# Feed-forward output of an encoder layer: sixteen of 22 row tiles by seven quadrant products per pair, partial sums kept in DRAM

## Chip, cores and metric

The kernel runs on one core of a Trainium2 chip. The core has TensorE (PE; PEld is its weight load), VectorE (DVE), ScalarE (ACT), GpSimd (POOL) and SyncE (SP), whose queue issues all the DMA transfers named here. The metric is device microseconds of one execution; each version is run several times, and the median is given.

## The reference, cut to what matters

One encoder layer is computed for two sequences of 512 tokens with a model width of 1024: a state-space branch, a differential-attention branch and a cross-attention branch, merged with gates, and a feed-forward part. All is in float32. The change touches only the last product:

```python
x = x + merged @ p['w_out'][l]
xn2 = _rmsnorm(x, p['norm_ffn'][l])
gate, up = jnp.split(xn2 @ p['w_ffn_in'][l], 2, axis=-1)
return x + (jax.nn.silu(gate) * up) @ p['w_ffn_out'][l]      # D_FF = 2816
```

After it `_rmsnorm(x, norm_final)` gives the output.

## The kernel before, in words

Features lie on the 128 partitions, the 1024 tokens of both sequences (NT) on the columns, 512 (L) per sequence. The feed-forward width of 2816 is KFF = 22 tiles of 128 rows; the output has KD = 8 tiles of rows, m = 0 to 7.

Float32 products are made from halves: `split` (L106) writes a rounded high half with ACT (L109, or L112 with a scale) and the rest, the low half, with DVE (L110 or L113). Each product of a 128x128 weight with 512 columns is then three matmuls: high by high, high by low, low by high (`mm3`, L124, and `product`, L732).

**First product (gate and up), L768 to L805.** It uses a seven-product scheme for 2x2 quadrants. One quadrant index is the sequence (columns 0:512 or 512:1024), the other on the input side is the upper or lower half of the eight input tiles (tiles i and i + 4), and on the output side the gate or the up tile. `operands` (L656) builds for each of four input pairs seven operands (four quadrants taken as they are or differenced with DVE and POOL, L663 to L666) and their high and low halves, in the buffers th0, tl0, th1, tl1 (two each, so four pairs fill them all). `weights4` (L677) loads the two weight tiles and forms four sums with POOL (L695 to L698) and splits all. One iteration has seven products (`SEVEN`, L741) of four k with three matmuls: 84 matmuls. `products` (L743) gives each a PSUM bank, in the middle iterations one product after the other; in the first and the last iteration k is the outer loop, with seven banks open. Sums of the products (`summed`, L776) are made by DVE from PSUM. Then the gate: DVE L800, L803, L804, ACT L801, POOL L802, and the tile of 128 x 1024 goes to DRAM (`aD`, L805).

**Second product, L825 to L867.** It is plain. The 22 row tiles are read back from `aD` in blocks of FBLK = 3, 5, 7 and 7 (L830) and split (L832) into "aa" or "ab" buffers. For each block and each m the weight columns are loaded and split (`weight`, L115), and `mm3` multiplies them with both sequences. The first block copies PSUM to `y` with ACT (L860), later ones add with DVE (L862); in the second block POOL adds the residual x1, which had been put into DRAM (L846, L847). The last block is done in three parts of columns (512, 256, 256) with its weights kept, so that the final norm of a part (`final`, L815, with sums of squares from L146) runs beside the next part.

**What sets the order.** The kernel is written with a tile framework: it takes the program's instructions with their dependencies and schedules them per engine at build time. At run time each engine's queue, SP's too, is in order, and an instruction that waits holds up all behind it. Buffers are pooled by tag: "ld" has four of 128 x 1024, "wf" two, the weight halves two each, "mm" six PSUM banks and "tr" two. A buffer is given out again when all its readers are done.

Of the kernel before, what the change touches and what calls it, by code (L numbers as in the profile page):

```python
# [10 lines left out]
F32 = mybir.dt.float32  # L11
# [18 lines left out]
T = 8  # L30
NC = L // T
G = 32
FBLK = (3, 5, 7, 7)


NG = (7, 5, 7)
# [12 lines left out]
def encoder(ctx: ExitStack, tc: tile.TileContext, a, out):  # L49
# [37 lines left out]
    def aux():  # L87
        return bank("tr")
# [556 lines left out]
    def out_tile(m, s, w):  # L645
# [7 lines left out]
        nc.sync.dma_start(x1D[m, :, cs], x1[m][:, cs])  # L653
        sum_sq(accs[s], x1[m][:, cs], m == 0)

    def operands(i):  # L656

        xa_, xb_ = x1[i], x1[i + 4]
        S.activation(out=xa_, in_=xa_, func=AF.Copy, scale=vcol("norm_ffn", i))
        V.tensor_scalar_mul(xb_, xb_, vcol("norm_ffn", i + 4))  # L660
        b11, b12, b21, b22 = xa_[:, 0:L], xa_[:, L:NT], xb_[:, 0:L], xb_[:, L:NT]
# [4 lines left out]
        V.tensor_tensor(out=t_[:, 3], in0=b21, in1=t_[:, 1], op=ALU.subtract)  # L666
        j = i // 2
        th, tl = slot(f"th{j}", [P, 7, L], F32R, "th"), slot(f"tl{j}", [P, 7, L], F32R, "tl")
        split(th[:, 0], tl[:, 0], b11)
        split(th[:, 1:3].rearrange("p a n -> p (a n)"), tl[:, 1:3].rearrange("p a n -> p (a n)"), xb_)  # L670
        split(th[:, 3:5], tl[:, 3:5], t_[:, 0:2])
        split(th[:, 5:7], tl[:, 5:7], t_[:, 2:4])
        return th, tl

    H = 4 * P

    def weights4(i):  # L677

        a1, a2 = (wp.tile([P, DM], F32, tag="wf", name="wf") for _ in range(2))
        nc.sync.dma_start(a1, a["w_fg"][i])  # L680
        nc.sync.dma_start(a2, a["w_fu"][i])
# [12 lines left out]
        s12, s34 = (slot("ws", name="ws") for _ in range(2))  # L694
        PO.tensor_tensor(out=s12[:, :H], in0=a2[:, :H], in1=a2[:, H:], op=ALU.add)  # L695
        PO.tensor_tensor(out=s12[:, H:], in0=s12[:, :H], in1=a1[:, :H], op=ALU.subtract)
        PO.tensor_tensor(out=s34[:, H:], in0=a1[:, H:], in1=s12[:, H:], op=ALU.subtract)
        PO.tensor_tensor(out=s34[:, :H], in0=a1[:, :H], in1=a2[:, :H], op=ALU.subtract)  # L698
        yield
        sp(ap2, s12, "s", "S1", "S2")  # L700
        sp(ap2, s34, "s", "S3", "S4")
        yield
# [14 lines left out]
            out_tile(m, s, w)  # L717
    phase.close()
    open_tags(phase, th1=2, tl1=2, ws=2)
    w0 = weights4(0)  # L720
    res0 = next(w0)
    next(w0)
    ops.append(operands(2))
    ops.append(operands(3))
    ses.close()
    ap2 = phase.enter_context(tc.tile_pool(name="ffn", bufs=1, reuse_waits="tile"))
    next(w0)

# [11 lines left out]

    SEVEN = (("A11", 0), ("S2", 4), ("A12", 1), ("S3", 5), ("S1", 3), ("A22", 6), ("S4", 2))  # L741

    def products(i, w):  # L743


        if i == 0:
            ps = [bank() for _ in range(6)]
            for j, k in ((0, 0), (0, 1), (1, 0), (1, 1), (0, 2), (1, 2), (0, 3), (1, 3)):
                for p_, (nm, o) in zip(ps, SEVEN):
                    if nm[0] == "AS"[j]:  # L750
                        product(p_, w[nm], o, (k,))
            yield from ps
            last = bank()
            product(last, w["S4"], 2)
            yield last
        elif i == KFF - 1:
            ps = [bank() for _ in range(6)] + [aux()]
            for k in range(4):
                for p_, (nm, o) in zip(ps, SEVEN):
                    product(p_, w[nm], o, (k,))  # L760
            yield from ps
        else:
            for nm, o in SEVEN:
                p_ = bank()
                product(p_, w[nm], o)
                yield p_

    for i in range(KFF):  # L768
        w = res0
        if i > 0:  # L770
            wg = weights4(i)
            w = next(wg)
            next(wg)
            next(wg)

        def summed(tag, p_, other, bufs=1):  # L776
            t_ = ap2.tile([P, L], F32, tag=tag, name=tag, bufs=bufs)
            V.tensor_tensor(out=t_, in0=p_, in1=other, op=ALU.add)  # L778
            return t_

        ps = products(i, w)
# [5 lines left out]
        p1 = ap2.tile([P, L], F32, tag="p1", name="p1")  # L787
        S.copy(p1, p0)
        u2 = summed("u2", next(ps), p1)
        gf0 = summed("gf", next(ps), p1, 2)  # L790
        u3 = summed("u3", next(ps), u2)
        p5 = next(ps)
        u4 = summed("p1", p5, u2)
        up1 = summed("up", p5, u3, 2)
        up0 = summed("up", next(ps), u3, 2)
        gf1 = summed("gf", next(ps), u4, 2)
        ac = ap2.tile([P, NT], F32, tag="ac", name="ac")
        for s, gf, up in ((0, gf0, up0), (1, gf1, up1)):
            cs = slice(s * L, (s + 1) * L)
            V.tensor_tensor(out=gf, in0=gf, in1=accs[s], op=ALU.mult)  # L800
            S.activation(out=ac[:, cs], in_=gf, func=AF.Tanh, scale=0.5)  # L801
            PO.tensor_tensor(out=up, in0=up, in1=accs[s], op=ALU.mult)  # L802
            V.scalar_tensor_tensor(out=ac[:, cs], in0=ac[:, cs], scalar=1.0, in1=gf, op0=ALU.add, op1=ALU.mult)  # L803
            V.tensor_tensor(out=ac[:, cs], in0=ac[:, cs], in1=up, op=ALU.mult)  # L804
        nc.sync.dma_start(aD[i], ac)  # L805
    phase.close()
    tes.close()


    open_tags(phase, yo=4)  # L810
    aes = ExitStack()
    open_tags(aes, side="right", aa=14, ab=14)
    y, y2 = [], []

    def final(acc, c0, n):  # L815
# [9 lines left out]
    f0 = 0  # L825
    for bi, nb in enumerate(FBLK):
        ah, al = [], []
        for i in range(f0, f0 + nb):
            ac = slot("ld", name="fl")
            nc.sync.dma_start(ac, aD[i])  # L830
            th, tl = (slot(("aa", "ab")[i // 7 % 2], [P, NT], F32R, n_) for n_ in ("ah", "al"))
            split(th, tl, ac, scale=0.5)  # L832
            ah.append(th)
            al.append(tl)
        last, kept = bi == len(FBLK) - 1, {}

        for parts in (((0, L),), ((L, L // 2),), ((L + L // 2, L // 2),)) if last else (((0, L), (L, L)),):
            acc = new_acc() if last else None
            for m in range(KD):
                if bi == 0:  # L840
                    if m % 2 == 0:
                        y2.append(slot("yo", [P, 2, NT], name=f"y{m}"))
                    y.append(y2[-1][:, m % 2])
                elif bi == 1:
                    xr = slot("ld", name="xr1")
                    nc.sync.dma_start(xr, x1D[m])  # L846
                    PO.tensor_tensor(out=y[m], in0=y[m], in1=xr, op=ALU.add)  # L847
                wsrc = a["w_fo"][m, :, f0 * P : (f0 + nb) * P]
                if not last:
                    wh, wl = weight(wsrc, nb * P)  # L850
                elif m in kept:
                    wh, wl = kept[m]
                else:
                    kept[m] = wh, wl = weight(wsrc, nb * P, "ab" if m < 6 else None)
                o = [bank()[:, :n] for _, n in parts]
                for k in range(nb):
                    mm3(o, wh, wl, [(ah[k][:, c : c + n], al[k][:, c : c + n]) for c, n in parts], k, nb)
                for o_, (c, n) in zip(o, parts):
                    if bi == 0:
                        S.copy(y[m][:, c : c + n], o_)  # L860
                    else:
                        V.tensor_tensor(out=y[m][:, c : c + n], in0=y[m][:, c : c + n], in1=o_, op=ALU.add)  # L862
                    if last:
                        sum_sq(acc, y[m][:, c : c + n], m == 0, n, V if m == KD - 1 else PO)
            if last:
                final(acc, *parts[0])
        f0 += nb  # L867

    phase.close()
    aes.close()  # L870
# [398 lines left out]
```

## Time and profile before

| | |
|---|---|
| runs of the kernel before | 1673.69 us median of 3 (1670.11 to 1674.54) |
| profiled execution: its time, its span | 1674.95 us, 1673.2 us |
| mean granted TensorE clock | 0.989 |
| first product: writes of its 22 tiles | issued from 1028.3 to 1433.7 us |
| second product and final norm | about 1418 us to the end |

The profile shows one execution. The page gives each engine's busy time and, at its part 4, the chain of work that ended last. Windows give busy time and counts by engine and stretch; the timeline lists instructions with start, duration, line, and output and input tiles; "x4" after a row means that many merged. A group's row gives its total us, the mean ns of one, and the idle time ahead of it with what ended it. Matmuls overlap, so a matmul's own duration is a latency; the distance from one to the next is what counts.

### The profile page before, as it was taken

How to read it: one execution, taken by the hardware profiler on the slowest of the kernel's cores; microseconds unless marked ns; L12 is line 12 of the kernel's file. 1: busy time of each engine (PE TensorE's matmuls, PEld its weight loads, DVE VectorE, ACT ScalarE, POOL GpSimd, SP SyncE). 2: the span in 40 equal slices, each digit the busy share in tenths (PEclk: the TensorE clock that was granted, in tenths of full speed). 3: DMA queues.
4: the chain of work that ended last, by engine and by line, in shares of the span. 5: the costliest groups of instructions: out<-in, count | busy, mean ns of one | idle time of the engine just before them, and what ended most of it. 6: DMA issues, size and time to landing. Idle time of an engine off the chain costs nothing.

```text
span 1673.2 us, 21052 instructions
## 1 busy us (share of the span) xinstructions
PE 1625.6 (97%) x7916; PEld 1357.8 (81%) x7916; DVE 1076.2 (64%) x1788; ACT 622.1 (37%) x1092; POOL 391.7 (23%) x253
## 2 busy tenths in 40 slices
PE   5999999999999999999999999999999999999997
PEld 4788887888897788878888878888888888888887
DVE  7946898154554776777655668777777777743324
ACT  6534412245343456554323443223323223421121
POOL 0001000000001121120243346555554552500021
PEclk9999999999999999999999999999999999999999
DMA  9343252747111221333554432322222223741302
GB/s 367 114 154 127 96 170 89 222 174 241 46 57 64 88 57 40 112 107 120 182 187 127 140 101 79 125 87 82 83 86 79 88 79 115 252 133 52 84 17 101
DMA packets 79269, 197.69 MB, mean 118 GB/s; under 512 B 11072, under 2 KB 26688, under 8 KB 79168
## 3 DMA queue, kind: packets, MB, share of 16 engines
q1 hardware_dynamic: 79168, 196.35, 35.4%
q8 instruction: 62, 1.02, 0.3%
q14 instruction: 39, 0.32, 0.1%
HBM read 141.82 MB, written 50.30 MB: 115 GB/s over the span
## 4 chain that ended last, share of the span: by engine, by line
PE 79%; DVE 11%; DMA 3%; issue 2%; ACT 2%; POOL 1%; SPq 1%; DVEq 0%; POOLq 0%; ACTq 0%
PE bkmm L129 15%; PE bkmm L132 15%; PE bkmm L130 15%; PE bkmm L738 8%; PE bkmm L737 8%; PE bkmm L739 8%; DVE st L1140 1%; DVE wl L110 1%; PE bktr L1122 1%; POOL mg L587 1%; PE bksc L533 1%; DMA c_n<-cD 1%; PE bksc L534 1%; PE bkmm L438 1%; PE bkmm L439 1%
## 5 line engine op out<-in xcount | busy, mean ns | idle before, releaser
L109 ACT CAST wh<-wf 128x1024 fp32r<-128x1024 f32 (+4 forms) x164 | 142.3, 868 | 385.4 <-PE bkmm L130 225.9
L132 PE MATMUL bkmm<-xh,wl 128*128 128x512 f32 x640 | 252.1, 394 | 3.0 <-DVE wl L110 3.0
L129 PE MATMUL bkmm<-xh,wh 128*128 128x512 f32 x640 | 251.8, 393 | 2.3 <-DVE t L505 1.2
L130 PE MATMUL bkmm<-xl,wh 128*128 128x512 f32 x640 | 251.7, 393 | 0.0
L738 PE MATMUL bkmm<-tl,wh 128*128 128x512 f32 x612 | 240.1, 392 | 2.5 <-DVE tl L110 2.5
L737 PE MATMUL bkmm<-th,wh 128*128 128x512 f32 x612 | 239.9, 392 | 0.0
L739 PE MATMUL bkmm<-th,wl 128*128 128x512 f32 x612 | 238.5, 391 | 0.0
L110 DVE TENSOR_TENSOR wl<-wf,wh 128x1024 fp32r<-128x1024 f32 (+4 forms) x164 | 175.7, 1072 | 94.5 <-ACT wh L109 93.9
L129 PE MATMUL bkmm<-ah,wh 128*128 128x512 f32 (+1 forms) x408 | 147.1, 361 | 0.2 <-ACT wh L109 0.2
L130 PE MATMUL bkmm<-al,wh 128*128 128x512 f32 (+1 forms) x408 | 147.0, 360 | 0.0
L132 PEld LDWEIGHTS bkmm<-xh,wl 128*128 128x128 f32 x640 | 120.7, 189 | 29.1 <-DVE wl L110 3.8
L129 PEld LDWEIGHTS bkmm<-xh,wh 128*128 128x128 f32 x640 | 120.7, 189 | 28.7 <-DVE t L505 2.6
L130 PEld LDWEIGHTS bkmm<-xl,wh 128*128 128x128 f32 x640 | 120.5, 188 | 24.7 <-issue 0.4
L506 POOL TENSOR_TENSOR t<-t,rs 128x512 f32<-128x512 f32 x16 | 24.6, 1537 | 494.5 <-DVE t L505 494.5
L738 PEld LDWEIGHTS bkmm<-tl,wh 128*128 128x128 f32 x612 | 115.8, 189 | 28.1 <-DVE tl L110 4.2
L737 PEld LDWEIGHTS bkmm<-th,wh 128*128 128x128 f32 x612 | 115.8, 189 | 24.4 <-ACT th L109 0.3
L739 PEld LDWEIGHTS bkmm<-th,wl 128*128 128x128 f32 x612 | 115.5, 189 | 24.0
L132 PE MATMUL bkmm<-ah,wl 128*128 128x512 f32 (+1 forms) x408 | 127.4, 360 | 0.5 <-DVE wl L110 0.4
L802 POOL TENSOR_TENSOR up<-up,acc 128x512 f32<-128x512 f32 x44 | 85.1, 1957 | 149.4 <-DVE up L778 149.4
L862 DVE TENSOR_TENSOR y<-y,bkmm 128x512 f32<-128x512 f32 (+1 forms) x56 | 32.6, 608 | 111.4 <-PE bkmm L132 111.4
L153 POOL TENSOR_TENSOR acc<-acc,nsq 128x512 f32<-128x512 f32 (+1 forms) x32 | 38.0, 1187 | 241.2 <-ACT nsq L152 241.1
L132 PEld LDWEIGHTS bkmm<-ah,wl 128*128 128x128 f32 x408 | 76.9, 189 | 12.7 <-DVE wl L110 1.3
(585 smaller groups left out, 3272.3 us busy)
## 6 DMA issues: line engine op xcount, KB each, us to landing
wf<-in_w_in SPq DMA_DIRECT2D x40, 512.0 KB, 3.8
gD<-gt SPq DMA_DIRECT2D x24, 512.0 KB, 2.8
gl<-gD SPq DMA_DIRECT2D x24, 512.0 KB, 3.9
wf<-in_w_fg SPq DMA_DIRECT2D x22, 512.0 KB, 3.7
wf<-in_w_fu SPq DMA_DIRECT2D x22, 512.0 KB, 3.7
aD<-ac SPq DMA_DIRECT2D x22, 512.0 KB, 2.6
fl<-aD SPq DMA_DIRECT2D x22, 512.0 KB, 4.5
wf<-in_w_fo SPq DMA_DIRECT2D x16, 448.0 KB, 3.3
```

The source lines that it names most:

```text
L109: S.copy(hi, src)
L110: V.tensor_tensor(out=lo, in0=src, in1=hi.bitcast(F32), op=ALU.subtract)
L129: PE.matmul(outs[s], wh[:, ws], xh, start=(k == 0), stop=False)
L130: PE.matmul(outs[s], wh[:, ws], xl, start=False, stop=False)
L132: last_mm = PE.matmul(outs[s], wl[:, ws], xh, start=False, stop=(k == nk - 1))
L153: eng.tensor_tensor(out=acc[:, :n], in0=acc[:, :n], in1=sq[:, :n], op=ALU.add)
L506: PO.tensor_tensor(out=t2, in0=t2, in1=rope[1], op=ALU.mult)
L737: PE.matmul(ps, wh[:, ws_], th[:, o], start=(k == 0), stop=False)
L738: PE.matmul(ps, wh[:, ws_], tl[:, o], start=False, stop=False)
L739: PE.matmul(ps, wl[:, ws_], th[:, o], start=False, stop=(k == 3))
L802: PO.tensor_tensor(out=up, in0=up, in1=accs[s], op=ALU.mult)
L862: V.tensor_tensor(out=y[m][:, c : c + n], in0=y[m][:, c : c + n], in1=o_, op=ALU.add)
```

## The change

The row tiles 0 to 15 go through the seven-product scheme too, in two blocks of eight tiles; the last six remain plain. In a block the quadrants of the weights are output tiles m or m + 4 by the first or last four of the block's row tiles; those of the rows are again the sequences and the pairs f, f + 4. A block has four iterations (m = 0 to 3), each with 84 matmuls as in the first product. `operands` is parted into `quad_sums` (the differences) and `quad_split` (the halves, now with a scale), and the pairs come from DRAM by `act_pair`. The differences of the first two pairs of a block are requested one iteration ahead, the other two at m = 0. With m = 0 and 3, and in the last iteration of the first product, k is the outer loop; its seven banks are now one "tr" bank first and then six "mm". What a block adds to starts with x1 in DRAM: an iteration reads the two tiles of the sum so far (`yp`, into "ld" buffers), POOL adds the four new quadrants to them, and each is written to new DRAM tiles (yb). The six plain tiles are done in the three parts of columns that the last block had before; `y` is now loaded from the second block's sums, and no longer starts as a copy. "aa" and "ab" have 12 buffers and not 14, "ts" two.

The core of the diff:

```diff
-FBLK = (3, 5, 7, 7)
+FW = 16
...
+    def quad_split(i, xa_, xb_, t_, scale=None):
+
         j = i // 2
         th, tl = slot(f"th{j}", [P, 7, L], F32R, "th"), slot(f"tl{j}", [P, 7, L], F32R, "tl")
+        split(th[:, 0], tl[:, 0], xa_[:, 0:L], scale)
+        split(th[:, 1:3].rearrange("p a n -> p (a n)"), tl[:, 1:3].rearrange("p a n -> p (a n)"), xb_, scale)
+        split(th[:, 3:5], tl[:, 3:5], t_[:, 0:2], scale)
+        split(th[:, 5:7], tl[:, 5:7], t_[:, 2:4], scale)
         return th, tl
...
-        elif i == KFF - 1:
-            ps = [bank() for _ in range(6)] + [aux()]
+        elif mode == "outer":
+            ps = [aux()] + [bank() for _ in range(6)]
...
+    def act_pair(f):
+
+        xa_, xb_ = slot("ld", name="fa"), slot("ld", name="fb")
+        nc.sync.dma_start(xa_, aD[f])
+        nc.sync.dma_start(xb_, aD[f + 4])
+        return xa_, xb_, quad_sums(xa_[:, 0:L], xa_[:, L:NT], xb_[:, 0:L], xb_[:, L:NT])
...
+        if i == KFF - 1:
+            acts = [act_pair(f) for f in range(2)]
...
+    for b in range(FW // 8):
+        f0 = 8 * b
+        fs = slice(f0 * P, (f0 + 8) * P)
+        for m in range(4):
+            wg = weights4(a["w_fo"][m, :, fs], a["w_fo"][m + 4, :, fs])
+            w = next(wg)
+            next(wg)
+            next(wg)
+            if m == 0:
+                ops = [quad_split(i, *acts[i], scale=0.5) for i in range(2)]
+                ops += [quad_split(i, *act_pair(f0 + i), scale=0.5) for i in (2, 3)]
+            if m == 3 and f0 + 8 < FW:
+                acts = [act_pair(f0 + 8 + i) for i in range(2)]
+            prior = []
+            for t in (m, m + 4):
+                prior.append(slot("ld", name="yp"))
+                nc.sync.dma_start(prior[-1], yb[b][t])
+            ps = products(w, "outer" if m in (0, 3) else None)
+            c11, c12, c21, c22 = quadrants(ps, next(ps))
+            for c_, t, s in ((c11, 0, 0), (c22, 1, 1), (c21, 1, 0), (c12, 0, 1)):
+                cs = slice(s * L, (s + 1) * L)
+                PO.tensor_tensor(out=c_, in0=c_, in1=prior[t][:, cs], op=ALU.add)
+                nc.sync.dma_start(yb[b + 1][m + 4 * t][:, cs], c_)
...
-    for bi, nb in enumerate(FBLK):
-        ah, al = [], []
-        for i in range(f0, f0 + nb):
...
+    nb = KFF - FW
+    ah, al = [], []
+    for i in range(FW, KFF):
+        ac = slot("ld", name="fl")
+        nc.sync.dma_start(ac, aD[i])
+        th, tl = (slot("aa", [P, NT], F32R, n_) for n_ in ("ah", "al"))
+        split(th, tl, ac, scale=0.5)
...
+    for c, n in ((0, L), (L, L // 2), (L + L // 2, L // 2)):
+        acc = new_acc()
+        for m in range(KD):
+            if c == 0:
...
+                nc.sync.dma_start(y[m], yb[-1][m])
+                kept.append(weight(a["w_fo"][m, :, FW * P :], nb * P, "ab" if m < 6 else None))
+            o = bank()[:, :n]
+            for k in range(nb):
+                mm3([o], *kept[m], [(ah[k][:, c : c + n], al[k][:, c : c + n])], k, nb)
+            V.tensor_tensor(out=y[m][:, c : c + n], in0=y[m][:, c : c + n], in1=o, op=ALU.add)
```

More of the change, by code (lines that the diff above doesn't have):

```diff
@@ L654, in out_tile, with quad_sums @@
         sum_sq(accs[s], x1[m][:, cs], m == 0)
[L656 to L661, printed above, removed]
+    def quad_sums(b11, b12, b21, b22):
         t_ = slot("ts", [P, 4, L], name="ts")
@@ L741, in encoder, with products @@
     SEVEN = (("A11", 0), ("S2", 4), ("A12", 1), ("S3", 5), ("S1", 3), ("A22", 6), ("S4", 2))
-    def products(i, w):
-        if i == 0:
+    def products(w, mode=None):
+        if mode == "first":
             ps = [bank() for _ in range(6)]
@@ L766, in products, with summed, quadrants @@
                 yield p_
+    def summed(tag, p_, other, bufs=1):
+        t_ = ap2.tile([P, L], F32, tag=tag, name=tag, bufs=bufs)
+        V.tensor_tensor(out=t_, in0=p_, in1=other, op=ALU.add)
+        return t_
+    def quadrants(ps, p0):
+        p1 = ap2.tile([P, L], F32, tag="p1", name="p1")
+        S.copy(p1, p0)
+        u2 = summed("u2", next(ps), p1)
+        c11 = summed("gf", next(ps), p1, 2)
+        u3 = summed("u3", next(ps), u2)
+        p5 = next(ps)
+        u4 = summed("p1", p5, u2)
+        c22 = summed("up", p5, u3, 2)
+        c21 = summed("up", next(ps), u3, 2)
+        return c11, summed("gf", next(ps), u4, 2), c21, c22
+    def act_pair(f):
[3 more added lines that the diff above has]
+        return xa_, xb_, quad_sums(xa_[:, 0:L], xa_[:, L:NT], xb_[:, 0:L], xb_[:, L:NT])
     for i in range(KFF):
@@ L774, in encoder @@
             next(wg)
[L776 to L781, printed above, removed]
+        if i == KFF - 1:
+            acts = [act_pair(f) for f in range(2)]
+        ps = products(w, "first" if i == 0 else "outer" if i == KFF - 1 else None)
         p0 = next(ps)
@@ L786, in encoder @@
                 S.copy(accs[s], bc)
[L787 to L796, printed above, removed]
+        gf0, gf1, up0, up1 = quadrants(ps, p0)
         ac = ap2.tile([P, NT], F32, tag="ac", name="ac")
@@ L805, in encoder @@
         nc.sync.dma_start(aD[i], ac)
+    yb = [[x1D[m] for m in range(KD)]] + [[drp.tile([P, NT], F32, name=f"y{b}D{m}") for m in range(KD)] for b in range(2)]
+    for b in range(FW // 8):
[21 more added lines that the diff above has]
+                nc.sync.dma_start(yb[b + 1][m + 4 * t][:, cs], c_)
     phase.close()
+    ses.close()
     tes.close()
@@ L823, in final @@
                 nc.sync.dma_start(out[c0 // L, :, m - 1 : m + 1, c0 % L : c0 % L + n], y2[m // 2][:, :, cs])
-    f0 = 0
-    for bi, nb in enumerate(FBLK):
-        ah, al = [], []
-        for i in range(f0, f0 + nb):
[L829 to L867, printed above, removed]
```

31 lines of the change are left out of this document (21 added, 10 removed).

## Prediction, written before the changed kernel ran

> **What bounds the kernel now.** The first page says which engine carries the end; then the windows of TensorE say how fast it goes where it waits for nothing, and where it loses time.
>
> ```profile
> span 1673.2 us, 21052 instructions
> ...
> PE 1625.6 (97%) x7916; PEld 1357.8 (81%) x7916; DVE 1076.2 (64%) x1788; ACT 622.1 (37%) x1092; POOL 391.7 (23%) x253
> ...
> PE 79%; DVE 11%; DMA 3%; issue 2%; ACT 2%; POOL 1%; SPq 1%; DVEq 0%; POOLq 0%; ACTq 0%
> ```
>
> ```profile
> 1100.00:1390.00 290.00, 290.00 (x1281) 1.00 0.24 84
> 1400.00:1410.00 10.00, 10.00 (x46) 1.00 0.13 52
> 1410.00:1420.00 10.00, 9.75 (x44) 1.00 0.77 258
> 1420.00:1430.00 10.00, 9.94 (x44) 1.00 0.48 158
> 1430.00:1440.00 10.00, 9.61 (x42) 1.00 0.75 264
> 1440.00:1450.00 10.00, 10.00 (x46) 1.00 0.77 257
> 1630.00:1650.00 20.00, 20.00 (x170) 1.00 0.28 107
> ```
>
> The columns are the stretch, its length and PE busy time (matmuls), granted clock, DMA share and GB/s. PE bounds the feed-forward part: 1281 matmuls in 290 us, one every 0.226 us (a group's mean of 0.39 us is a latency; matmuls overlap). Of 256 columns one starts every 20/170 = 0.118 us. From 1410 to 1440, where the first product becomes the second, 8 matmuls fewer than 46 per window start: before loses 8 x 0.226 = 1.8 us there. So whatever saves matmuls saves time only as long as operands come as fast.
>
> **What the change removes.** Before multiplies 15 tiles of rows as 720 matmuls of 512 columns, and the last seven as 168 of 512 and 336 of 256. Afterwards the sixteen tiles are two blocks of four pairs of output tiles, 7 products x 4 x 3 = 84 matmuls each: 672; the last six tiles are 144 of 512 and 288 of 256. Gone are 72 x 0.226 + 48 x 0.118 = 16.3 + 5.6 = **21.9 us**. The 1.8 us go too, since that seam is replaced: 23.7 us is all that there is to win.
>
> **What it adds, in the middle of a block.** To price it, durations and pitches:
>
> ```profile
> 1355.46 0.69 DVE L778 TENSOR_TENSOR p<-bkmm,u 128x512 f32<-128x512 f32 x1 [1.69 <-PE bkmm L739]
> 1356.07 0.68 DVE L778 TENSOR_TENSOR up<-bkmm,u 128x512 f32<-128x512 f32 x1
> 1356.66 1.21 DVE L110 TENSOR_TENSOR wl<-ws,wh 128x1024 fp32r<-128x1024 f32 x1
> ...
> 1409.70 4.63 DVE L113 SCALAR_TENSOR_TENSOR al<-fl,ah 128x1024 fp32r<-128x1024 f32 x4 [6.38 <-PE bktr L739]
> ```
>
> ```profile
> 1344.48 1.54 POOL L695 TENSOR_TENSOR ws<-wf 128x512 f32<-128x512 f32 x1 [2.80 <-ACT ac L801]
> ...
> 1344.79 1.78 DVE L803 SCALAR_TENSOR_TENSOR ac<-ac,gf 128x512 f32<-128x512 f32 x1
> 1346.10 1.62 POOL L696 TENSOR_TENSOR ws<-ws,wf 128x512 f32<-128x512 f32 x1
> ...
> 1346.61 1.67 DVE L804 TENSOR_TENSOR ac<-ac,up 128x512 f32<-128x512 f32 x1
> 1347.68 1.74 POOL L698 TENSOR_TENSOR ws<-wf 128x512 f32<-128x512 f32 x1
> 1348.20 0.68 DVE L778 TENSOR_TENSOR u<-bkmm,p 128x512 f32<-128x512 f32 x1
> ...
> 1349.39 1.29 POOL L697 TENSOR_TENSOR ws<-wf,ws 128x512 f32<-128x512 f32 x1
> ```
>
> A DVE instruction of 512 columns follows the last after 0.60 us (1355.46, 1356.07, 1356.66), one of 1024 after 1.14 (four take 4.63 = 3 x 1.14 + 1.21). The second fence shows POOL and DVE taking turns: an L803 that needs 0.68 us takes 1.78 beside L695, the next DVE instruction 1.67, and POOL's own spans stretch by as much. Only L778, whose first input lies in PSUM, keeps its 0.68. Four POOL additions and two such DVE instructions fill 1344.48 to 1350.68: (6.2 - 2 x 0.68) / 4 = 1.2 us for a POOL addition alone. So I count 1.2 us of DVE delay per POOL addition that meets DVE work from SBUF. The Trainium skill states as much (SBUF — State Buffer, "SBUF: two separate sides"): DVE with two SBUF inputs and GpSimd take one port pair by an exclusive lock. By that rule the delay is whole and not shared out, which is the forecast and not the second rival below; the trace agrees, with 1.78 us where 0.68 would do.
>
> A pair in mid-block (19.0 us of PE: 84 x 0.226) needs from DVE four weight splits (3 x 1.14 + 0.7) and seven sums from PSUM (7 x 0.6): 8.3 us; from POOL four weight sums and four additions of earlier partial sums, 8 x 1.2 = 9.6. What excludes each other is 4.1 + 9.6 = 13.7 us: hidden. DMA moves two weights, two partial sums in and four halves out, 3.1 MB per 19 us = 165 GB/s, under the 264 of the window at 1430: hidden too. If this cover failed: third rival.
>
> **The two seams where a block starts.**
>
> ```profile
> L110 DVE TENSOR_TENSOR wl<-wf,wh 128x896 fp32r<-128x896 f32 x16 | 17.4, 1088 | 10.5 <-ACT wh L109 10.5
> L109 ACT CAST wh<-wf 128x896 fp32r<-128x896 f32 x16 | 15.1, 945 | 76.2 <-PE bkmm L130 69.6 <-DMA wf<-in_w_fo 6.6
> L112 ACT ACTIVATE ah<-fl 128x1024 fp32r<-128x1024 f32 x22 | 23.1, 1061 | 19.5 <-DMA fl<-aD 11.1 <-PE bktr L738 5.2 <-PE bktr L739 1.9
> L109 ACT CAST wh<-wf 128x512 fp32r<-128x512 f32 x22 | 13.7, 623 | 34.0 <-PE bkmm L738 32.7 <-PE bkmm L130 1.3
> ```
>
> The number behind the bar is total us, then mean ns. Here the sixteen operands' halves are made: per operand tile one split of 512 and three of 1024 columns and three differences on DVE, a fourth difference on POOL. Buffers for them come free only as the last products of the block before end with one k after another. Time is counted from the first matmul of that last iteration (order of L756 to L761, now also taken for m = 3). In the built order the first buffer is free after 35 matmuls, 7.9 + 0.4 us; ACT's first high half takes 0.6, so DVE begins at 9.0. PE can only go on into the second pair (its second product, 182nd matmul, at 182 x 0.226 = 41.2 us if nothing waits) after DVE has done, in its order, everything up to that pair's weight split.
>
> First seam: 44 DVE instructions (17 of 1024, 27 of 512 columns; among them the sums of both iterations and the gate's) are 17 x 1.14 + 27 x 0.60 = 35.6 us, plus 0.5 for ACT's second copy. Nine POOL additions stand between (two differences, four weight sums, two products of L802, one partial sum): 9 x 1.2 = 10.8, less 1.8 that lies beside three sums from PSUM. 9.0 + 0.5 + 35.6 + 9.0 = 54.1, so PE loses **12.9 us**.
>
> Second seam (block to block): the sums of the first two operands are done before it, and no gate; 38 instructions (17 and 21) are 32.0 us. DVE begins 1.6 later behind POOL's weight sums and the second operand's differences; eleven POOL additions cost 13.2 less 1.8. 9.0 + 1.6 + 0.5 + 32.0 + 11.4 = 54.5: **13.3 us** lost. Both are bounded below by no collision at all (54.1 - 9.0 and 54.5 - 13.0: 3.9 and 0.3 us lost) and above by loads that come late: I take them as free because DVE is late anyway; one landing (4.5 us, row below) each if not.
>
> **The third seam, into the six plain tiles.**
>
> ```profile
> aD<-ac SPq DMA_DIRECT2D x22, 512.0 KB, 2.6
> fl<-aD SPq DMA_DIRECT2D x22, 512.0 KB, 4.5
> ```
>
> Four "ld" buffers serve six row tiles, and partial sums share them. In the built order the sixth load waits for the fourth tile's low half, and that for the last drains, which start after the block's matmuls end at 19.0 us; SP issues it at 23.5, behind five 512 KB loads of y. Landing is 28 (4.5 us) if these do not count, 20.3 + 6 x 0.52 MB / 264 GB/s = 32.2 if they queue; I take 30. ACT does the sixth high half (1.1) and only then the first weight (945 ns x 768/896 = 0.8), DVE the sixth low half (1.2) and the first weight's (1088 ns x 768/896 = 0.9): PE's long run begins at 33.2, with 0.9 us done of it before. 33.2 - 19.0 - 0.9 = **13.3 us** lost (11 to 15.5).
>
> **The clock.** Before has one stall of this sort, where its own four operands are made:
>
> ```profile
> 990.00:995.00 5.00, 3.45 (x16) 1.00 0.52 186
> 995.00:1000.00 5.00, 4.68 (x19) 0.61 0.00 0
> 1000.00:1005.00 5.00, 3.74 (x10) 0.50 0.01 2
> 1005.00:1010.00 5.00, 5.00 (x13) 0.52 0.02 5
> 1010.00:1015.00 5.00, 5.00 (x23) 1.00 0.62 193
> ```
>
> ```profile
> 1004.25 0.63 PE L739 MATMUL bkmm<-th,wl 128*128 128x512 f32 x1
> 1004.68 0.63 PE L737 MATMUL bkmm<-th,wh 128*128 128x512 f32 x1
> 1005.11 0.63 PE L738 MATMUL bkmm<-tl,wh 128*128 128x512 f32 x1
> ```
>
> After the gaps of 990 to 1000 the clock falls to 0.50 and a matmul starts every 0.43 us until about 1009.5: 5.6 us at half pace, 2.8 lost. I take 2.8 for the third seam, whose gap is whole, and half of it for the others, whose gaps are broken up by short runs: 5.6 us (0 to 8.4). The Trainium skill (TensorE: Matmul & The Clock Gate, "Part 1: The HAM clock gate") has the full clock back after some 3.4 us of work; as an estimate from that page, three seams would cost 3 x 1.7 = 5.1 us. The row shows a longer time, and the sum goes by the row.
>
> **Sum.** 12.9 + 13.3 + 13.3 + 5.6 = 45.1 added, 23.7 gone: +21.4 us on the profiled execution's 1674.95, 1696.4. The median of the runs shown is 1.3 lower, so **1695 us**; with the bounds of the seams above, 1684 to 1706.
>
> **Rivals.** (1) *The seams of the blocks are hidden.* Per k PE has 21 matmuls = 4.75 us, one operand's splits take DVE 4.0 (0.6 + 3 x 1.14), so operands arrive in step and only the third seam stays: 13.3 + 2.8 - 23.7 = -7.6, 1666 us: faster. It decides from where all stalls together stay under 23.7 us. For it: the orders are interleaved by k for this. Against it: DVE has differences, drains and two pairs' weights in the same queue. (2) *POOL does not delay DVE*: 3.9 + 0.3 + 13.3 + 2.8 - 23.7 = -3.4, 1670: no change. Against it: the rows at 1344. (3) *Worse*: the clock stays at 0.5 through each long catch-up (55 matmuls from the drain of the fourth product to the 182nd, 55 x 0.2 = 11 us, 8 more than counted, twice) and the sixth load queues (+2.2): 1712. For it: each seam's 13 us come as a few gaps and not as many small ones, since PE waits for whole banks and splits. (4) *The middle of a block does not keep PE's pace*: SP's queue is in order, and weights stand behind writes that wait for POOL's additions. Two us for each of six pairs: 1707.
>
> **How the numbers follow.** Forecast 0.60, (1) 0.08, (2) 0.09, (3) 0.15, (4) 0.08. A measurement can tell about 0.3% here, 5.0 us: faster 0.08, the same 0.09, slower 0.60 + 0.15 + 0.08 = 0.83. The range leaves out (1) and (2), 0.17, and reaches to (3): 1676 to 1712.
>
> **What would show it.** Right: in the profile after, PE windows of 84 matmuls in 19 us in mid-block, and three stretches with missing matmuls of 13 to 16 us each; DVE without a gap from some 9 us into the last gate iteration, with waits of PE on DVE's low halves (L113, L110) and POOL between; before the first plain matmul a gap that ends with ACT's weight copy behind the sixth row tile's load; clocks under 1 behind each. Wrong: DVE with idle time in the block seams (rival 1), L113 at 1.22 us beside POOL (rival 2), or mid-block pairs longer than 19.3 us (rival 4).

## The result and the profile after

The changed kernel takes 1696.85 us (median of 4 runs, 1693.99 to 1698.30) against 1673.81 us before: 1.0135 times as long, 95% interval 1.0122 to 1.0148. The forecast was 1695. The profiled execution took 1695.88 us, with a span of 1694.1 and a mean clock of 0.982 (before: 1674.95, 1673.2, 0.989).

The page of after, the lines that answer to those of before:

```profile
span 1694.1 us, 21125 instructions
...
PE 1613.3 (95%) x7796; PEld 1343.6 (79%) x7796; DVE 1161.9 (69%) x1860; ACT 641.1 (38%) x1108; POOL 498.5 (29%) x317
...
PE 77%; DVE 14%; DMA 3%; issue 2%; ACT 2%; POOL 1%; SPq 0%; DVEq 0%; POOLq 0%; ACTq 0%
```

There are 120 matmuls fewer (7796 for 7916), just those that the scheme saves, and DVE's share of the chain has grown from 11 to 14%, POOL's instructions from 253 to 317. Where PE stands still shows in the windows of after. The columns are stretch, length, busy time (and count) of PE, PEld, DVE, ACT and POOL, granted clock, DMA share, GB/s:

```profile
1350.00:1400.00 50.00, 50.00 (x222) 41.42 (x221) 37.75 (x46) 15.61 (x19) 25.37 (x15) 1.00 0.25 84
1410.00:1460.00 50.00, 42.97 (x170) 33.07 (x169) 49.95 (x51) 21.92 (x27) 23.11 (x13) 0.93 0.46 149
1460.00:1500.00 40.00, 40.00 (x179) 33.11 (x178) 24.54 (x25) 11.82 (x14) 34.98 (x22) 1.00 0.57 192
1500.00:1550.00 50.00, 39.51 (x156) 30.59 (x155) 49.65 (x48) 19.15 (x23) 26.11 (x16) 0.93 0.57 186
1550.00:1590.00 40.00, 40.00 (x179) 33.11 (x178) 19.35 (x21) 9.02 (x10) 25.74 (x16) 1.00 0.54 182
1590.00:1630.00 40.00, 24.28 (x101) 19.64 (x100) 18.70 (x21) 11.37 (x15) 7.92 (x5) 0.83 0.69 236
```

An undisturbed stretch holds 222 matmuls in 50 us (first row) and 179 in 40 us (third and fifth row, the middles of the two blocks). The three seams miss 222 - 170 = 52, 222 - 156 = 66 and 179 - 101 = 78 matmuls; at 0.2264 us (290 us / 1281, a row of before) these are **11.8, 14.9 and 17.7 us**, 44.4 in all. Less the 23.7 us that the change saves, that is +20.7; the spans differ by 20.9. So the three seams are the whole difference, and the middles of the blocks cost nothing. In the windows of the first two seams DVE is busy for 49.95 and 49.65 of 50 us; in the third it is not (18.70 of 40), and the DMA share is 0.69. Ahead of the second window DVE does stand still: from 1490.5 to 1497.1 it waits 4.34 and 1.57 us for two row tiles (`fa` and `fb` of the second pair), whose loads (issued at 1489.8 and 1492.1) stand on SP behind writes of sums that POOL had to finish first.

The longest waits of PE between 1400 and 1640 in after (total us, times, longest):

```profile
PE bkmm L129 <- ACT wh L109: 15.7, 1, 15.7
PE bkmm L745 <- ACT wh L109: 4.2, 1, 4.2
PE bkmm L746 <- DVE tl L113: 3.7, 3, 2.6
PE bkmm L745 <- DVE u L778: 3.5, 1, 3.5
```

One long wait (third seam, L129 is the first plain matmul), and several short ones, whose ends are weights, operands and sums in turn: the picture of a queue that is late as a whole.

DVE and POOL in the second seam of after:

```profile
1521.69 1.46 POOL L702 TENSOR_TENSOR ws<-wf 128x512 f32<-128x512 f32 x1 [6.11 <-DMA wf<-in_w_fo]
1521.92 2.30 DVE L113 SCALAR_TENSOR_TENSOR tl<-ts,th 128x1024 fp32r<-128x1024 f32 x1
1523.10 2.28 POOL L705 TENSOR_TENSOR ws<-wf 128x512 f32<-128x512 f32 x1
1524.15 1.77 DVE L113 SCALAR_TENSOR_TENSOR tl<-fa,th 128x512 fp32r<-128x512 f32 x1
1525.34 1.74 POOL L851 TENSOR_TENSOR up<-up,yp 128x512 f32<-128x512 f32 x1
1525.85 2.31 DVE L113 SCALAR_TENSOR_TENSOR tl<-ts,th 128x1024 fp32r<-128x1024 f32 x1
1527.04 2.27 POOL L703 TENSOR_TENSOR ws<-ws,wf 128x512 f32<-128x512 f32 x1
1528.08 1.77 DVE L661 TENSOR_TENSOR ts<-fb,ts 128x512 f32<-128x512 f32 x1
```

Behind the first row nothing waits for data here, yet each DVE instruction of 512 columns takes 1.77 us and each of 1024 takes 2.30, where 0.68 and 1.22 do without POOL. POOL's rows stretch too, up to 2.28 us. The DVE instructions begin 2.23, 1.70 and 2.23 us apart instead of 1.14, 0.60 and 1.14: 1.1 us more for each POOL instruction.

The third seam in after: load of the sixth row tile, ACT behind it, the first plain matmuls, and two windows of 5 us:

```profile
1598.36 2.85 SPq L889 DMA_DIRECT2D y<-y1D  x5
...
1601.78 0.97 SPq L875 DMA_DIRECT2D fl<-aD  x1
...
1611.28 1.06 ACT L112 ACTIVATE ah<-fl 128x1024 fp32r<-128x1024 f32 x1 [8.71 <-DMA fl<-aD]
...
1613.11 0.80 PE L129 MATMUL bkmm<-ah,wh 128*128 128x512 f32 x1 [15.72 <-ACT wh L109]
...
1615.83 0.58 PE L130 MATMUL bkmm<-al,wh 128*128 128x512 f32 x1
1616.26 0.39 PE L132 MATMUL bkmm<-ah,wl 128*128 128x512 f32 x1
```

```profile
1605.00:1610.00 5.00, 0.00 (x0) 0.00 (x0) 0.00 (x0) 0.00 (x0) 0.00 (x0) 0.50 1.01 365
1610.00:1615.00 5.00, 1.89 (x5) 1.48 (x6) 2.63 (x3) 2.51 (x3) 0.00 (x0) 0.50 0.92 319
```

For five microseconds PE, DVE, ACT and POOL stand still, and the DMA engines are full (share 1.01, 365 GB/s): the sixth load, issued at 1601.8 behind five loads of y, is used by ACT at 1611.3, 9.5 us later. PE then starts one matmul every 0.43 us until 1616.3.

### The profile page after: what moved, and what is told of

Same layout as the page of the kernel before. It is cut to its first block, busy times and chain, and to the rows that moved or that the text cites. A ratio compares the mean times of both kernels' runs of the same rounds, so it can differ in the third digit from the quotient of the medians.

```text
span 1694.1 us, 21125 instructions
## 1 busy us (share of the span) xinstructions
PE 1613.3 (95%) x7796; PEld 1343.6 (79%) x7796; DVE 1161.9 (69%) x1860; ACT 641.1 (38%) x1108; POOL 498.5 (29%) x317
## 4 chain that ended last, share of the span: by engine, by line
PE 77%; DVE 14%; DMA 3%; issue 2%; ACT 2%; POOL 1%; SPq 0%; DVEq 0%; POOLq 0%; ACTq 0%
PE bkmm L129 13%; PE bkmm L130 12%; PE bkmm L132 12%; PE bkmm L746 9%; PE bkmm L747 9%; PE bkmm L745 9%; DVE wl L110 2%; DVE tl L113 2%; DVE st L1169 1%; PE bktr L1151 1%; PE bksc L533 1%; PE bksc L534 1%; PE bkmm L438 1%; PE bkmm L440 1%; PE bkmm L439 1%
## 5 line engine op out<-in xcount | busy, mean ns | idle before, releaser
L745 PE MATMUL bkmm<-th,wh 128*128 128x512 f32 x820 | 321.8, 394 | 10.7 <-ACT wh L109 4.2
L746 PE MATMUL bkmm<-tl,wh 128*128 128x512 f32 x820 | 322.7, 394 | 7.6 <-DVE tl L110 3.9
L747 PE MATMUL bkmm<-th,wl 128*128 128x512 f32 x820 | 319.2, 392 | 0.9 <-DVE wl L110 0.9
L129 PE MATMUL bkmm<-xh,wh 128*128 128x512 f32 x640 | 252.4, 394 | 1.1 <-DVE vl L110 1.0
L109 ACT CAST wh<-wf 128x1024 fp32r<-128x1024 f32 (+2 forms) x156 | 137.3, 881 | 296.7 <-PE bkmm L130 133.5
L110 DVE TENSOR_TENSOR wl<-wf,wh 128x1024 fp32r<-128x1024 f32 (+2 forms) x156 | 173.0, 1110 | 91.0 <-ACT wh L109 90.5
L129 PEld LDWEIGHTS bkmm<-xh,wh 128*128 128x128 f32 x640 | 121.4, 190 | 27.1 <-DVE vl L110 1.6
L109 ACT CAST wh<-ws 128x1024 fp32r<-128x1024 f32 x60 | 63.0, 1051 | 135.7 <-PE bkmm L746 90.2
L110 DVE TENSOR_TENSOR wl<-ws,wh 128x1024 fp32r<-128x1024 f32 x60 | 78.8, 1314 | 6.5 <-ACT wh L109 6.5
L702 POOL TENSOR_TENSOR ws<-wf 128x512 f32<-128x512 f32 x30 | 53.4, 1781 | 80.3 <-DMA wf<-in_w_fu 43.2
L366 DVE TENSOR_REDUCE nb<-bksc 128x1 f32<-128x512 f32 (+1 forms) x96 | 55.9, 592 | 30.1 <-PE bksc L465 18.0
L130 PE MATMUL bkmm<-yl,wh 128*128 128x512 f32 x192 | 75.2, 392 | 0.6 <-DVE yl L113 0.6
```

Of the source, the lines that this page charges most:

```text
L109: S.copy(hi, src)
L110: V.tensor_tensor(out=lo, in0=src, in1=hi.bitcast(F32), op=ALU.subtract)
L129: PE.matmul(outs[s], wh[:, ws], xh, start=(k == 0), stop=False)
L130: PE.matmul(outs[s], wh[:, ws], xl, start=False, stop=False)
L366: V.tensor_reduce(out=nb, in_=sc, axis=AX.X, op=ALU.max, negate=True)
L745: PE.matmul(ps, wh[:, ws_], th[:, o], start=(k == 0), stop=False)
```

## The experiments

Theory on the way in: the first two seams are DVE's queue, lengthened by each POOL instruction that meets it (**operands and lock**); the third is the "ld" buffers and the loads of y that stand ahead of the sixth row tile (**loads**). Rivals: POOL is no burden to DVE; the seams are loads or drains and not the making of operands; the parts are not independent.

Nine kernels were run, all beside the kernel before. Ratios are to it; differences in us are differences of ratios by 1675, good to about 3 us against after and 2 among those with more runs. "Lost" is worked out as above, from the profile of each kernel, in stretches of the same lengths.

| kernel | ratio, 95% interval | against after | lost in seams 1, 2, 3 (us) | sum less 23.7 | span less 1673.2 |
|---|---|---|---|---|---|
| after | 1.0135 [1.0122, 1.0148] | | 11.8, 14.9, 17.7 | +20.7 | +20.9 |
| e1_y_late | 1.0112 [1.0097, 1.0127] | -3.9 | 12.0, 15.2, 16.3 | +19.8 | +21.5 |
| e2_dve_adds | 1.0079 [1.0064, 1.0094] | -9.4 | 9.5, 9.5, 18.8 | +14.1 | +14.4 |
| e3_reuse | 1.0037 [1.0025, 1.0049] | -16.4 | 9.7, 0, 18.1 | +4.1 | +4.0 |
| e4_ld_free | 1.0052 [1.0036, 1.0067] | -13.9 | 11.3, 13.6, 7.5 | +8.7 | +7.4 |
| e5_both | 1.0024 [1.0015, 1.0033] | -18.6 | 9.3, 10.4, 9.1 | +5.1 | +5.1 |
| e6_reuse_both | 0.9969 [0.9958, 0.9981] | -27.8 | 0, 0, 18.1 | -5.6 | -6.6 |
| e7_gate | 1.0020 [1.0010, 1.0029] | -19.3 | 8.4, 10.2, 8.4 | +3.3 | +6.4 |
| e8_last_pool | 1.0024 [1.0015, 1.0033] | -18.6 | 9.1, 9.5, 9.5 | +4.4 | +2.4 |
| e9_last_pool_gate | 1.0024 [1.0015, 1.0033] | -18.6 | 8.4, 9.5, 10.0 | +4.2 | +2.8 |

Lost time and span agree within 1.7 us in eight of ten rows, and within 3.1 in all.

**e1_y_late**: the loads of y are issued after the sixth row tile's.

```diff
-        nc.sync.dma_start(ac, aD[i])
+        last_fl = nc.sync.dma_start(ac, aD[i])
...
-                nc.sync.dma_start(y[m], yb[-1][m])
+                with tc.issue_after(last_fl.ins):
+                    nc.sync.dma_start(y[m], yb[-1][m])
```

> Seam into the plain tiles alone: the loads of y are queued on SP behind the sixth row tile's load; nothing else is changed. In the profile after, that load was issued at 1601.8 us and landed 9.5 us later, with five loads of y ahead of it. Theory (the loads of y hold it up): it lands after about 4.5 us, TensorE resumes 5 us earlier, the time falls by 4 to 6 us against the changed kernel (about 1692 us), the other two seams unchanged. Rival (the wait for the buffer and the load's own landing set it): less than 1 us, about 1697.

Measured: 1694.92 us; -3.9 by the ratios, just short of the 4 to 6 of the theory and with an interval that nearly touches 0. The third seam of its profile loses only 1.4 us less. PE's waits from 1590 to 1630, and the loads of the next weights in e1:

```profile
PE bkmm L129 <- ACT wh L109: 12.1, 3, 9.9
```

```profile
1613.62 9.66 SPq L117 DMA_DIRECT2D wf<-in_w_fo  x4
...
1620.17 1.76 ACT L109 CAST wh<-wf 128x768 fp32r<-128x768 f32 x2 [3.34 <-DMA wf<-in_w_fo]
```

The long wait shrank from 15.7 to 9.9 us, as the loads theory has it; but the loads of y now fill the queue ahead of the third weight, which ACT can copy only at 1620, and PE waits twice more (2.2 us). Behind each of the two gaps PE runs at half pace for a while, and its 107 matmuls from 1590 to 1630 take 27.9 us where 24.2 would do. So most of the gain went into a new wait on the same queue and the slow stretch behind it.

**e2_dve_adds**: the partial sums of all pairs, the fourth difference of the operands and the weight sums of m = 1 go from POOL to DVE.

```diff
-    def quad_sums(b11, b12, b21, b22):
+    def quad_sums(b11, b12, b21, b22, eng=PO):
...
-        PO.tensor_tensor(out=t_[:, 2], in0=b22, in1=b12, op=ALU.subtract)
+        eng.tensor_tensor(out=t_[:, 2], in0=b22, in1=b12, op=ALU.subtract)
...
-            wg = weights4(a["w_fo"][m, :, fs], a["w_fo"][m + 4, :, fs])
+            wg = weights4(a["w_fo"][m, :, fs], a["w_fo"][m + 4, :, fs], V if m == 1 else PO)
...
-                PO.tensor_tensor(out=c_, in0=c_, in1=prior[t][:, cs], op=ALU.add)
+                V.tensor_tensor(out=c_, in0=c_, in1=prior[t][:, cs], op=ALU.add)
```

> In the two block seams POOL's additions are given to DVE: all additions of earlier partial sums, the fourth operand difference, and the four weight sums of m = 1 of each block. So 7 of 9 POOL operations leave the first seam and all 11 the second; DVE has 7 and 11 instructions of 0.6 us more. Theory (a POOL operation holds DVE up for 1.2 us): 7 x (1.2 - 0.6) = 4.2 less in the first seam, 11 x 0.6 = 6.6 less the 1.8 that lay beside PSUM sums = 4.8 less in the second: about 9 us faster than the changed kernel, 1688. Rival (POOL costs DVE nothing, DVE's own work is all): 18 x 0.6 = 10.8 us slower, 1708.

Measured: 1689.22 us, -9.4. The same DVE group in after and in e2 (ns min/median/max), then the windows of e2:

```profile
L113 DVE SCALAR_TENSOR_TENSOR tl<-ts,th x16: 1207/1216/2322, 1409.9 to 1540.0; 128x1024 fp32r<-128x1024 f32 x16
```

```profile
L113 DVE SCALAR_TENSOR_TENSOR tl<-ts,th x16: 1215/1222/1233, 1409.7 to 1532.3; 128x1024 fp32r<-128x1024 f32 x16
```

```profile
1410.00:1460.00 50.00, 45.21 (x180) 34.73 (x179) 48.63 (x63) 21.75 (x27) 4.58 (x3) 0.93 0.52 175
1500.00:1550.00 50.00, 43.42 (x180) 34.08 (x179) 47.21 (x64) 18.61 (x22) 5.30 (x4) 0.97 0.65 210
1580.00:1620.00 40.00, 23.60 (x96) 19.04 (x95) 19.12 (x24) 11.12 (x13) 0.00 (x0) 0.79 0.62 223
```

DVE, the engine that is late, got 12 and 16 instructions *more* in these stretches, and the seams became 2.3 and 5.4 us shorter. An addition of 512 columns costs DVE 0.6 us when it makes it itself, and 1.1 when POOL makes it beside it as in the rows at 1521; the stretched durations (maximum 2322 ns) are gone (1233). A POOL that cost DVE nothing would have made this kernel slower, 0.6 us for each addition. The rival fell. The theory's shares were less exact than its sum: it had 4.2 us for the first seam, where 2.3 came. And 1.0 of the second seam's 5.4 us is not DVE's own work: DVE began the halves 12.5 us after the first matmul of m = 3 (1484.68 to 1497.19) and not 13.5 as in after (1487.05 to 1500.57), since the writes ahead of the row tiles' loads no longer wait for POOL (the second pair's last load was issued 3.5 us after that matmul and not 5.0).

**e3_reuse** and **e6_reuse_both**: the second block (e3), or both (e6), multiply operands that are there already.

```diff
-            if m == 0:
+            if m == 0 and b == 0:
                 ops = [quad_split(i, *acts[i], scale=0.5) for i in range(2)]
                 ops += [quad_split(i, *act_pair(f0 + i), scale=0.5) for i in (2, 3)]
-            if m == 3 and f0 + 8 < FW:
-                acts = [act_pair(f0 + 8 + i) for i in range(2)]
```

e6 leaves out these lines altogether, and the request of the first two pairs in the last gate iteration.

> The second block multiplies the operands of the first again: its row tiles are not loaded, no differences and no halves are made for it (so half of the product is computed from the wrong rows). Orders of products, weights, drains and partial sums stay. Theory (making the operands costs the second seam its 15.2 us, 67 matmuls fewer than undisturbed): the seam goes to under 1 us, the time falls by 14 to 15 us to about 1682. Rival (the k-outer order, its open banks and its drains at the end cost a good part): 7 us or more of the seam stay, 1689 or more.

> Neither block makes operands: both multiply those of the first product again (so the product is computed from the wrong rows for sixteen tiles); no loads, differences and halves for them. Theory (making operands is what the first seam costs too): against the run that reused them in the second block only, 11 to 12 us less, the 53 matmuls that the first seam lacked coming back but for a few; about 1669, faster than the kernel before by some 6 us. Rival (the first seam is long because of the last gate, which is still there, and the k-outer order): less than 6 us less, 1675 or more.

Measured: 1680.47 us (-16.4) and 1669.23 us (-27.8, another -11.4). Windows of the first two seams in e3, and of e6 with the third:

```profile
1410.00:1460.00 50.00, 43.08 (x179) 32.43 (x178) 47.94 (x52) 21.49 (x27) 32.60 (x13) 1.00 0.50 160
...
1500.00:1550.00 50.00, 50.00 (x222) 41.43 (x221) 33.36 (x35) 13.15 (x17) 35.14 (x24) 1.00 0.57 190
```

```profile
1410.00:1460.00 50.00, 50.00 (x222) 41.43 (x221) 37.78 (x39) 14.34 (x18) 29.45 (x19) 1.00 0.42 137
1500.00:1550.00 50.00, 50.00 (x222) 41.42 (x221) 30.96 (x33) 11.81 (x14) 34.81 (x24) 1.00 0.56 183
1565.00:1605.00 40.00, 23.90 (x99) 19.31 (x98) 18.18 (x20) 11.85 (x15) 7.03 (x5) 0.79 0.68 234
```

Where no operands are made, PE does its 222 matmuls with weights, drains, partial sums and their loads all in place, so none of these makes the two seams by itself. The two edits take out the row tiles' loads, the differences and the halves together; that DVE's part of them decides, more than the loads, rests on DVE's 49.95 and 49.65 busy us of 50 in after. What is left in e6 is the third seam, 18.1 us, against 23.7 won: -5.6, and -5.2 (ratio 0.9969) was measured. It is the only kernel under the time of before, and it leaves out what the scheme needs.

e3 also shows a limit of the 1.1 us. Its first seam is that of after, unchanged, and yet lost 9.7 us and not 11.8. POOL's two differences there, and DVE's splits beside the first of them, in after and then in e3 (first the two differences' ns min/median/max):

```profile
1414.06 1.66 POOL L660 TENSOR_TENSOR ts<-fb,fa 128x512 f32<-128x512 f32 x1 [6.07 <-DVE tl L113]
...
1414.48 3.45 DVE L113 SCALAR_TENSOR_TENSOR tl<-ts,th 128x1024 fp32r<-128x1024 f32 x2
```

```profile
L660 POOL TENSOR_TENSOR ts<-fb,fa x2: 5697/6384/7072, 1414.1 to 1419.7; 128x512 f32<-128x512 f32 x2
```

```profile
1413.94 2.35 DVE L113 SCALAR_TENSOR_TENSOR tl<-ts,th 128x1024 fp32r<-128x1024 f32 x2
```

In after each difference held DVE up by 1.1 us (two splits in 3.45 us here, one in 2.29 beside the other difference). In e3 POOL was the one that waited: by its rows the differences took 5.7 and 7.1 us, and DVE's splits kept 2.35 and 1.22 us. e4 has the same (5.9 and 7.1 us). What decides which of the two waits was not tried. So some 2 us of e3's gain do not come from the reuse.

**e4_ld_free**: in the last pair of the second block the sums so far are read into a "ts" buffer, so that the "ld" buffers are free for the row tiles; the loads of y stand behind the fourth weight's.

```diff
-                prior.append(slot("ld", name="yp"))
+                if b == 1 and m == 3:
+                    if t == m:
+                        both = slot("ts", [P, 4, L], name="yq")
+                    prior.append(both[:, 2 * (t // 4) : 2 * (t // 4) + 2].rearrange("p a n -> p (a n)"))
+                else:
+                    prior.append(slot("ld", name="yp"))
...
-    kept = []
+    kept = [weight(a["w_fo"][m, :, FW * P :], nb * P, "ab" if m < 6 else None) for m in range(4)]
...
-                nc.sync.dma_start(y[m], yb[-1][m])
+                with tc.issue_after(gate_w.ins):
+                    nc.sync.dma_start(y[m], yb[-1][m])
```

(`gate_w` is the fourth weight's load.)

> Seam into the plain tiles, further than with the late loads of y: the last pair's partial sums are read into a free ts buffer instead of two ld buffers, so that all six row tiles can be loaded before the block ends, and y is loaded behind the fourth weight. Theory (buffers and queue order make this seam): the gap of 15.9 us before the first plain matmul goes; what comes next is the third weight, queued behind the writes of the last sums that wait for POOL, a gap of about 4 us. Of 17.7 us some 5 stay: 12 to 13 us faster than the changed kernel, about 1685. Rival (DVE's and ACT's splits and the last drains set the seam): no more than the 5 us of the late loads of y, about 1692.

Measured: 1685.03 us, -13.9. The third seam's window in e4:

```profile
1580.00:1620.00 40.00, 35.81 (x146) 27.66 (x145) 19.61 (x22) 13.26 (x17) 10.12 (x6) 0.96 0.61 220
```

33 matmuls are missing instead of 78, 7.5 us for 17.7: most of the third seam's price was the loads. PE still waits 4.2 us there (2.2 for DVE's low half of a weight, 2.0 for ACT's copies), in all about the size of the gap of 4 us that was expected.

**e5_both** is e2 and e4 together.

> DVE in POOL's place in the block seams, and the free buffers with late loads of y at the third seam, in one kernel. Theory (the seams are separate and each is set by its own cause): the two gains add, 9.4 + 13.9 = 23.3 us less than the changed kernel, which is the whole of what it lost: within 3 us of the kernel before (ratio 0.998 to 1.002). Rival (they share a cause, so the second gains less, as when DVE with POOL's work is late for the third seam's splits): 5 us or more above before.

Measured: 1679.07 us, -18.6, still 0.24% (4.0 us) over before: less than the bound of 0.3%, but the interval leaves out 1. That lies between the 3 us of the theory and the 5 of the rival. The two gains do not quite add up (9.4 + 13.9 = 23.3). The third seam in e5 (L859 is the addition, L110 the weight's low half):

```profile
1593.98 1.29 DVE L859 TENSOR_TENSOR up<-up,yq 128x512 f32<-128x512 f32 x2
1595.18 0.69 DVE L859 TENSOR_TENSOR gf<-gf,yq 128x512 f32<-128x512 f32 x1
1595.78 1.83 DVE L110 TENSOR_TENSOR wl<-wf,wh 128x768 fp32r<-128x768 f32 x2
...
1596.80 0.80 PE L135 MATMUL bkmm<-ah,wl 128*128 128x512 f32 x1 [4.21 <-DVE wl L110]
```

DVE has the block's last additions ahead of the first plain weight, and PE waits 4.2 us for it. Behind the wait PE runs at half pace until 1602.9, for 6.1 us, where in e4 it was 3.4 (1598.2 to 1601.6).

**e7_gate** is e5 with the two gate products of the last iteration on DVE.

```diff
-            PO.tensor_tensor(out=up, in0=up, in1=accs[s], op=ALU.mult)
+            (V if i == KFF - 1 else PO).tensor_tensor(out=up, in0=up, in1=accs[s], op=ALU.mult)
```

> As the kernel with both remedies, and the two POOL products of the last gate iteration, which lie in the first seam, are done by DVE too. Theory (1.2 us of delay for a POOL operation against 0.6 for a DVE instruction): 1.2 us faster than with both remedies. Rival: no change, or 1.2 us slower if POOL was beside PSUM sums there.

Measured: 1678.41 us, -0.7 against e5 with intervals that overlap: nothing can be concluded.

**e8_last_pool** is e5 with the last pair's additions back on POOL, and **e9_last_pool_gate** is the same with e7's edit.

```diff
-                V.tensor_tensor(out=c_, in0=c_, in1=prior[t][:, cs], op=ALU.add)
+                (PO if b == 1 and m == 3 else V).tensor_tensor(out=c_, in0=c_, in1=prior[t][:, cs], op=ALU.add)
```

> This is e5_both with the four last additions of partial sums (second block, m = 3) back on POOL; everything else as there. Theory (in e5 the third seam ended with DVE, which had four additions of 0.6 us ahead of the first plain weight's low half): up to 4 x 0.6 = 2.4 us of the gap before the first plain matmul go, and half a us of the clock with it: -1.5 to -2.9 us against e5_both's 1679.1, so 1676.2 to 1677.6, about 2 us over the kernel before. Rival (a POOL addition beside DVE's weight splits delays them by 1.2 us each, as in the seams of the blocks): no gain or a loss of up to 2.4 us, 1679 to 1681.5.

> This is e8_last_pool with the two products of the last gate iteration (L802 in the kernel before) on DVE too, as in e7_gate. Theory: the same 0.7 to 1.2 us less as e7_gate had against e5_both, 1675 to 1677: about as fast as the kernel before, but not under it by what can be told. Rival: no difference from e8_last_pool.

Measured: 1678.99 and 1679.28 us, both with e5's ratio. The theory missed, the rival's time came. PE's waits in e8 from 1580 to 1620, and what DVE, SP and ACT did (L860 writes the block's result, L120 loads a weight):

```profile
PE bkmm L132 <- ACT wh L109: 2.5, 3, 1.1
PE bkmm L135 <- DVE wl L110: 2.2, 2, 1.9
```

```profile
1590.20 2.99 DVE L110 TENSOR_TENSOR wl<-wf,wh 128x768 fp32r<-128x768 f32 x2
...
1592.35 1.99 POOL L859 TENSOR_TENSOR gf<-gf,yq 128x512 f32<-128x512 f32 x1
1594.36 0.32 SPq L860 DMA_DIRECT2D y1D<-gf  x1
1594.77 0.89 SPq L120 DMA_DIRECT2D wf<-in_w_fo  x2
...
1599.27 0.83 ACT L109 CAST wh<-wf 128x768 fp32r<-128x768 f32 x1 [10.65 <-DMA wf<-in_w_fo]
```

The wait on DVE did shrink, 4.2 to 2.2 us (the two low halves now take 2.99 us instead of 1.83, beside POOL). In its place the next weights came late: their loads stand on SP behind the write of POOL's last addition, 1594.4, and PE waits 2.5 us for ACT's copies of weights (0.9 in e5). So 5.1 us of waiting (4.2 and 0.9) became 4.7, and PE's half pace behind the shorter wait lasted 6.1 us (1591.3 to 1597.4), as long as in e5. e9 gives the same time; an effect of the gate's products can be told neither there nor in e7.

No kernel that computes all of it beats the one before.

## Why the prediction was right, step by step

Where PE goes on behind the second pair's weight splits, in the first and in the second seam of after:

```profile
1451.99 0.50 PE L747 MATMUL bkmm<-th,wl 128*128 128x512 f32 x1 [0.40 <-DVE wl L110]
...
1539.53 0.50 PE L747 MATMUL bkmm<-th,wl 128*128 128x512 f32 x1 [0.50 <-DVE wl L110]
```

- **What is won**: 120 matmuls and the old seam, 23.7 us. The count is exact, and with it the lost time gives the spans as closely as the table shows.
- **First seam**: forecast 12.9 for DVE and 1.4 for the clock, measured 11.8. From the first matmul of the last gate iteration (1398.98 in the trace) DVE was to be through with the second pair's weight split at 54.1; PE went on behind it at 1451.99, after 53.0. DVE began at 8.8 (forecast 9.0), the 44 instructions are exact, and POOL cost some 8 us of the 9.0 counted. The 1.4 us of clock did not come in after: the stretches at half pace lie ahead of 1452, and PE still had to wait for DVE there (0.40 us; in e3, without such a stretch, 1.54 us at the same place). A slow PE costs nothing more where it has to wait anyway, and the prediction counted it on top. But where the slow stretch falls is luck: in e4 DVE was 2.2 us earlier, because the two differences did not hold it up, and the half pace came behind the same wait (1448.1 to 1451.5) and cost 1.6 us, so that its first seam lost 11.3.
- **Second seam**: forecast 13.3 + 1.4, measured 14.9; the size is right because errors cancel, which is luck. DVE began the halves 13.5 us after the first matmul of m = 3 and not 10.6: the row tiles' loads, which were taken as free, came late. From there to the second pair's weight split it needed 38.9 us and not 43.9, with 35 instructions instead of 38 and 9.8 us of delays instead of 11.9. So it was through after 52.5 us (1487.05 to 1539.5) and not 54.5, but only 167 matmuls had been started by then, where the working had the 182nd as the one that waits.
- **A POOL instruction costs DVE 1.2 us**: 1.1 in the rows at 1521, and e2 turned its sign into a test. The Trainium skill (SBUF — State Buffer, "SBUF: two separate sides") has the lock; the trace agrees. The price is not paid each time: in the first seam of e3 and e4 two splits beside POOL's differences kept their 1.2 us each, the sign that the prediction had given for rival 2, and POOL waited.
- **Third seam**: forecast 13.3 + 2.8, measured 17.7. The load was issued at 23.6 us after the block's last iteration began (1597.2, the end of its last matmul, less 84 x 0.2264 = 1578.2; forecast 23.5). The step that was off is the landing: 30 was taken, 28 if the loads of y do not count and 32.2 if they queue; ACT used the tile at 33.1, beyond the upper bound. The queue is real, and the DMA engines also carried the block's last writes. The clock's part is 1.6 and not 2.8: half pace for 3.2 us (1613.1 to 1616.3). The Trainium skill (TensorE: Matmul & The Clock Gate, "Part 1: The HAM clock gate") has some 3.4 us; the third seam of after agrees with it; the row of before (5.6 us), by which the sum went, and e5 and e8 (6.1 us) do not.
- **Middle of the blocks**: full pace (179 in 40 us, clock 1.00), so rival 4 fell. Rival 1 fell with DVE's 49.95 and 49.65 of 50 us, though DVE did stand still ahead of the second window; rival 2 fell with e2. Rival 3's queued load came, its clock did not.

In all 45.1 us were forecast for the seams and 44.4 came: first -2.5, second +0.2, third +1.6. That the sum is so close is in part luck, since these errors have both signs: the prediction asked for three stretches of 13 to 16 us each, and only the second seam lies in that.

Three slips of the working do not touch the forecast. With its own lower bounds (3.9, 0.3 and 11, and 5.6 for the clock) the low end is 1671 and not 1684. Rival 3, with 11 us in place of 1.4 in two seams and 2.2 for the load, comes to 1716 and not 1712. For the middle of a block the text points at the third rival and means the fourth.

Why e5 gains 4.7 us less than e2 and e4 apart is told only in part. In the third seam e5 lost 1.6 us more than e4; its rows show 0.9 us more of waiting, and a longer stretch at half pace. e8, which gives the last additions back to POOL, does not win it back (9.5 us lost). The second seam's 0.9 and the rest are within what runs differ.

## What to carry to other kernels

A scheme that saves matmuls is paid for where its operands are made: per block of 8 row tiles it saved 48 matmuls (10.9 us) here, and a seam in which DVE must make the operands of four pairs costs 8 to 15 us, so compare these two first, per block. When DVE is the late engine, moving SBUF additions to POOL need not be relief (1.1 us of delay for 0.6 us of work in after); time them beside each other before dividing the work. And at a change of phase follow each load on the in-order queue: whichever load was put first, the one behind it became the next wait (e1, e8).

## What the hardware showed that was not expected

- One 512 KB load took 9.5 us to its use behind five others and some writes, with the DMA share at 1.01 and 365 GB/s; the median of such loads in after is 4.5.
- Half pace of PE lasted 5.6 us in the kernel before. Behind the wait in the third seam it lasted 3.2 us in after (a wait of 15.7 us), 3.4 in e4 (2.0), and 6.1 in e5 (4.2) and in e8 (1.9), so the length of the wait does not tell it. What makes the difference was not tried.
- The same two POOL differences beside the same DVE splits held DVE up by 1.1 us each in after, and held up nothing in e3 and e4, where they took 5.7 to 7.1 us themselves.
